# Doubling the recurrence tiles of a hybrid decoder layer, storing branch results in DRAM, and re-tiling its small matrix products

## The chip, the cores and the metric

The kernel runs on one core of a Trainium2 chip. The metric is the device time of one execution in microseconds (us); a time without other words is the median of several executions. A profile is one further execution, recorded instruction by instruction.

## The reference, cut to what matters

One layer on x of 512 tokens by 2048 channels: h = RMSNorm(x), one input projection `h @ w_in` to 57 column tiles of 128, three branches, a SiLU gate on each, one output projection, and the residual.

```python
pa, pb, pc = split(h @ w_in)
# A: RWKV-7, 12 heads of 64; per token t, state S (64 x 64):
#    sa = S @ (-kk_t);  S = S*w_t + outer(sa, kk_t*a_t) + outer(v_t, k_t);  y_t = S @ r_t
#    then group norm of y, plus bonus = sum(r*k*r_k) * v, times silu(ga)
# B: trailing means over 2/4/8/16 tokens minus the token, a 128x128 map per group, a scale, times silu(pg)
# C: stick-breaking attention, 12 heads of 64, QK-norm, strictly causal:
#    z = q @ k.T;  w = exp(log_sigmoid(z) + reversed cumsum of log_sigmoid(-z));  o = w @ v, times silu(g)
out = x + concat(A, B, C) @ w_out
```

## The kernel before

**Layout.** Channels lie on the 128 partitions and the 512 tokens on the free axis. A "pair" is two heads of 64, the lower one (`lo`) on partitions 0 to 63 and the upper one (`hi`) on 64 to 127. There are six pairs for branch A, six for branch C and four groups for branch B.

**Projections.** Each operand of the two big projections is split into a high and a low part of type float32r, and `three` issues three products per block of 128 rows: high-high, high-low and low-high. One column tile of the input projection is thus 16 x 3 = 48 products of 128x128 by 512 columns, into a PSUM bank called `pj`. The first three tiles go into banks called `first` while x arrives; the other 54 tiles follow in a fixed order, eight for a pair (k, r, v, ga, cq, ck, cv, cg), at the end eight for the pooling groups. The output projection is 4 x 4 x 16 x 3 = 768 such products into banks called `oacc`. Weights stream in by half tiles: a 512 KB load (`raw`, two buffers, queue of SyncE, SP), a cast on ScalarE (ACT) that gives `wh`, and a subtraction on VectorE (DVE) that gives `wl`, two buffers each.

**The order on TensorE (PE).** `project` issues the products of one column tile after another, and after each product it calls `pump`. Branches are generators (`rwkv(p)`, `attention(p)`, `pooling(g)`) that stop at `yield need(...)`. A planner (`Pace`) models when each tile will be ready and when a bank of a tag will be free; `pump` resumes a generator once the modelled time has passed that by a margin (MARGIN 1.5 us, TIGHT 0.05 us in the recurrence). Small products of a branch are in this way strewn among the big ones, and all engines work in the order in which they were issued.

**Branch A, pair p.** Decay (`dec`) and rate (`av`) from two products each, the second of which uses 64 rows alone; a sum of squares (`ss`). Chunks of 64 tokens: `bk` holds the keys of the pair and `amr` the decayed keys and receptances. `gm`, four products for each half sequence and head with 64 rows, 128 columns of weights and 128 moving columns, gives the triangles `lt`, `rx` and a part of `amr`. The triangles are inverted: four 32-row pieces go to DRAM, come back so that 128 of them lie on the partitions, a loop of 30 steps on DVE solves them, they go back, and two rounds of 32x32 products (`q`) finish. Then come eight chunks in a row, each with five products per head: `w` (64 output columns of the array), copy to `wsb`, `u` (64x64), copy to `uv`, `s` (64 output columns), the new state into `uv` with the help of `se`, and two products into `y`. A head's product uses its own half of the array. Group norm (`mu`, `var`) and the gate follow. There is one set of `bk`, `amr`, `lt`, `rx`, `ec`, so `rwkv(p)` waits for the end of the recurrence of p-1 before it writes them.

**Branch C, pair p.** QK-norm (`qm`), then per head: scores `z` in three banks, each piece as one product with all 128 rows (high and low part of q stacked) and one with 64 rows (low part of k); an exponential, a scan and POOL's (GpSimd's) masks; ten transposes (`wT`) of the weights into one tile; and four products into `o`, which use 64 output columns.

**Results** of all branches stay in SBUF, one tile each (`yt`), until the output projection, which begins once all tasks but one are done. PSUM banks: two `pj`, three `g` (all phase products), three `c` (recurrence).

Every product is issued by one helper, line 350 (transposes: 354), every DVE, ACT and POOL instruction by line 198, every DMA by line 212 on SP, so rows are told apart by the tiles' names. A float32 product stands as two instructions in the profile, a float32r product and a transpose as one:

```python
pe.matmul(o, lhsT, rhs, start=start, stop=stop)      # line 350, in mm()
pe.transpose(o, src, ident)                          # line 354
call(*args, **kw)                                    # line 198, DVE, ACT and POOL
queue.dma_start(out=out, in_=in_)                    # line 212, SP
```

Of the kernel before, what the change touches and what calls it, by code (L numbers as in the profile page):

```python
# [8 lines left out]
F32 = mybir.dt.float32  # L9
# [4 lines left out]
P = 128  # L14
# [38 lines left out]
BANKS = {"pj": 2, "g": 3, "c": 3}  # L53
MARGIN = 1.5
TIGHT = 0.05
AHEAD = 300
EVACUATE = 25
DL = 4.0


def tile_order():
    tiles = [("wdad", 0)]
    for p in range(NPAIR):
        tiles += [("k", p), ("r", p), ("v", p), ("ga", p)]
        tiles += [("cq", p), ("ck", p), ("cv", p), ("cg", p)]
    for g in range(NPOOL):
        tiles += [("pu", g), ("pg", g)]
    return tiles
# [18 lines left out]
Y_TILE = {("a", i): i for i in range(6)} | {("b", i): 6 + i for i in range(4)} | {("c", i): 10 + i for i in range(6)}  # L87


class Pace:  # L90
# [37 lines left out]
    def cost(self, eng, f, out, ins):  # L128
# [3 lines left out]
        if eng == "pool":  # L132
            if f in ("memset", "affine_select"):
                return 0.05 + n * 0.0011
            return 0.08 + n * (0.0028 if f == "tensor_scalar" else 0.0033)
        if f in ("tensor_scalar", "tensor_copy", "memset") and not any(self.key(a) in self.read_psum for a in ins):
            n *= 0.5
        return 0.065 + n * 0.00104
# [13 lines left out]
    def matmul(self, out, lhsT, rhs):  # L152
        n = self.free(rhs)
        m = self.free(lhsT)
        if rhs.dtype == F32R:
            c = max(n / 2400.0, m * 0.00083)
        else:
            c = max(4 * max(n, 64) / 2400.0, 0.1) * (0.6 if m <= 64 or rhs.shape[0] <= 64 else 1.0)
# [45 lines left out]
def hybrid_trunk_kernel(ctx: ExitStack, tc: tile.TileContext, x, xT, w_in, w_out, vecs, consts, up_w, pool_w, out, tap=None):  # L204
# [15 lines left out]
    tp = ctx.enter_context(tc.tile_pool(name="tp", bufs=14))  # L220
# [57 lines left out]

    hh = [hp.tile([P, T], F32R, tag=f"hh{k}", name=f"hh{k}") for k in range(KT)]
# [14 lines left out]
    for pl, tag, parts in ((ap, "q2", 1), (ap, "k2", 1), (ap, "w3", 1), (rp, "bk", 2), (rp, "bkt", 2), (rp, "rx", 2),  # L294
                           (rp, "uv", 2), (rp, "amr", 3), (ap, "wt", 2)):
        xt = pl.tile([P, parts, T], F32, tag=tag, name=name("x"))
# [15 lines left out]
    def row_sums():  # L312
        for i in range(8):
            xs = yp.tile([P, D // 2], F32, tag="y12" if i % 2 == 0 else "y14", name=name("xs"))
# [43 lines left out]
    def need(*tiles, tag=None, margin=MARGIN):  # L358
        def at():
            t = max([pace.ready.get(Pace.key(a), 0.0) for a in tiles] + [0.0])  # L360
            return margin + (max(t, pace.bank_at(tag, BANKS[tag])) if tag else t)

# [115 lines left out]

    yt = {}
    ypair = {}  # L480

    def ytile(branch, i):
        n = Y_TILE[(branch, i)]
        if n >= 12:
            if n - n % 2 not in ypair:
# [566 lines left out]
```

## Time and profile before

| | |
|---|---|
| median of 3 runs | 1093.07 us (1091.02 to 1093.6) |
| the profiled execution | 1089.68 us, span in the trace 1088.0 us |
| granted TensorE clock, mean | 0.993 |
| busy: PE, DVE, ACT, POOL | 1066.2, 737.6, 427.8, 143.1 us |
| PE instructions | 5552 products, of which 2592 `pj`, 768 `oacc`, 144 `first` |
| DMA | 101.92 MB, mean 94 GB/s |

The span has three stretches: to about 42 us the `first` tiles, to 908 us the input projection with the branches in it, then the output projection. In the middle stretch the work repeats every 130 us, once a pair; 485 to 615 us is one such period. Busy time of PE counts each product until its modelled end, so products overlap in it; what a product costs is read from the starts.

### The profile page before, as it was taken

The numbers are of one execution on the slowest core, as the hardware profiler recorded it, in microseconds if no ns is written. First come the engines' busy times: TensorE is split into PE (matmuls) and PEld (weight loads), VectorE is DVE, ScalarE is ACT, GpSimd is POOL, SyncE is SP. The second block draws the span as 40 slices with busy tenths as digits, with TensorE's granted clock in tenths as the row PEclk, the third lists the DMA queues.
The fourth block names the chain that finished last, engine by engine and source line by source line (L and its number), as shares of the span: only waits on it lengthen the run. The fifth ranks groups of instructions, "written<-read, shape, count | busy, mean of one in ns | idle before, by whom it ended". The sixth has DMA issues, their size and how long they took to land.

```text
span 1088.0 us, 14731 instructions
## 1 busy us (share of the span) xinstructions
PE 1066.2 (98%) x5552; PEld 801.3 (74%) x5552; DVE 737.6 (68%) x1596; ACT 427.8 (39%) x670; POOL 143.1 (13%) x208
## 2 busy tenths in 40 slices
PE   9998999999999999999999999999999999999998
PEld 7877766687666877668766787667776677888887
DVE  6266978759787797778877799777986457223232
ACT  6453525235353354334543345524443235111111
POOL 0031113101132011210211102210021111000000
PEclk9999999999999999899999999999999999999999
DMA  9513231132211321113221132112221125444232
GB/s 329 204 63 105 80 93 40 56 92 84 84 48 51 107 85 66 58 59 97 86 76 39 64 115 77 61 58 84 100 78 55 48 94 163 149 154 137 96 137 75
DMA packets 58185, 101.92 MB, mean 94 GB/s; under 512 B 29312, under 2 KB 30720, under 8 KB 58112
## 3 DMA queue, kind: packets, MB, share of 16 engines
q1 hardware_dynamic: 58112, 100.96, 28.2%
q8 instruction: 44, 0.72, 0.3%
q14 instruction: 29, 0.24, 0.1%
HBM read 95.17 MB, written 5.77 MB: 93 GB/s over the span
## 4 chain that ended last, share of the span: by engine, by line
PE 80%; DVE 10%; issue 4%; ACT 2%; DMA 2%; POOL 2%; SPq 0%; POOLq 0%; DVEq 0%; ACTq 0%
PE pj L350 45%; PE oacc L350 15%; PE first L350 3%; PE o L350 2%; PE z L350 2%; DVE w L198 2%; DVE wl L198 2%; PE gm L350 2%; PE y L350 2%; PE w L350 2%; PE wT L354 1%; DVE xblk L198 1%; PE u L350 1%; POOL e L198 1%; PE s L350 1%
## 5 line engine op out<-in xcount | busy, mean ns | idle before, releaser
L350 PE MATMUL pj<-hl,wh 128*128 128x512 f32 x864 | 349.0, 404 | 0.0
L350 PE MATMUL pj<-hh,wh 128*128 128x512 f32 x864 | 347.9, 403 | 1.0 <-DVE u L198 0.8
L350 PE MATMUL pj<-hh,wl 128*128 128x512 f32 x864 | 347.6, 402 | 0.0
L198 DVE TENSOR_TENSOR wl<-raw,wh 128x1024 fp32r<-128x1024 f32 x140 | 172.1, 1229 | 168.6 <-ACT wh L198 162.8
L198 ACT CAST wh<-raw 128x1024 fp32r<-128x1024 f32 x140 | 147.0, 1050 | 312.7 <-PE pj L350 187.5
L350 PEld LDWEIGHTS pj<-hh,wh 128*128 128x128 f32 x864 | 163.1, 189 | 38.0 <-issue 4.4
L350 PEld LDWEIGHTS pj<-hh,wl 128*128 128x128 f32 x864 | 163.2, 189 | 35.4 <-issue 0.4
L350 PEld LDWEIGHTS pj<-hl,wh 128*128 128x128 f32 x864 | 163.1, 189 | 35.5 <-issue 1.2
L350 PE MATMUL oacc<-wl,yh 128*128 128x512 f32 x256 | 100.1, 391 | 0.8 <-DVE wl L198 0.8
L350 PE MATMUL oacc<-wh,yl 128*128 128x512 f32 x256 | 99.6, 389 | 0.0
L350 PE MATMUL oacc<-wh,yh 128*128 128x512 f32 x256 | 99.6, 389 | 0.0
L198 POOL TENSOR_SCALAR e<-e 128x512 f32<-128x512 f32 x28 | 49.0, 1749 | 327.9 <-ACT e L198 327.6
L198 POOL TENSOR_TENSOR d<-u 128x512 f32<-128x512 f32 x25 | 34.2, 1370 | 230.9 <-DVE u L198 148.6
L350 PEld LDWEIGHTS oacc<-wl,yh 128*128 128x128 f32 x256 | 48.0, 188 | 11.5 <-DVE wl L198 1.3
L350 PEld LDWEIGHTS oacc<-wh,yl 128*128 128x128 f32 x256 | 48.1, 188 | 10.0 <-issue 0.2
L350 PEld LDWEIGHTS oacc<-wh,yh 128*128 128x128 f32 x256 | 48.0, 188 | 10.0
L198 DVE TENSOR_TENSOR xblk<-xblk,pr 128x60 f32<-128x60 f32 (+8 forms) x180 | 44.5, 247 | 4.1
L198 ACT ACTIVATE e<-e 128x512 f32<-128x512 f32 x50 | 31.4, 629 | 39.1 <-POOL e L198 38.8
L198 DVE TENSOR_TENSOR_SCAN w<-kon,n 128x512 f32<-128x512 f32 (+3 forms) x48 | 39.3, 841 | 6.6 <-POOL n L198 6.5
L198 DVE TENSOR_TENSOR pr<-xblk,nblk 128x60 f32<-128x60 f32 (+8 forms) x180 | 38.7, 215 | 4.4
L198 DVE TENSOR_TENSOR u<-pj,rstd 128x512 f32<-128x512 f32 x50 | 34.3, 686 | 8.3 <-PE pj L350 7.9
L198 ACT ACTIVATE n<-n 128x512 f32<-128x512 f32 (+1 forms) x72 | 38.9, 557 | 1.3
(195 smaller groups left out, 1262.7 us busy)
## 6 DMA issues: line engine op xcount, KB each, us to landing
raw<-in_w_in SPq DMA_DIRECT2D x108, 512.0 KB, 3.4
raw<-in_w_out SPq DMA_DIRECT2D x32, 512.0 KB, 3.4
xs<-in_x SPq DMA_DIRECT2D x8, 512.0 KB, 4.7
xr<-in_x SPq DMA_DIRECT2D x16, 256.0 KB, 5.3
out<-xr SPq DMA_DIRECT2D x16, 256.0 KB, 3.2
fr<-in_w_in SPq DMA_DIRECT2D x12, 256.0 KB, 7.4
nblk<-s SPq DMA_DIRECT2D x24, 128.0 KB, 4.9
x<-in_xT SPq DMA_DIRECT2D x5, 512.0 KB, 7.4
```

Source lines behind the costliest of these rows:

```text
L198: return call(*args, **kw)
L350: pe.matmul(o, lhsT, rhs, start=start, stop=stop)
L354: pe.transpose(o, src, ident)
```

## The change

- Two sets of `amr`, `lt`, `bk`, `rx`, `ec` and `bv`, used in turn; `rwkv(p)` waits for the recurrence of p-2 before it writes them, and for that of p-1 only before its own recurrence. `bkt`, `uv`, `yc` stay single.
- `amr` has four 64-column parts a chunk, the third zero on the upper, the fourth zero on the lower partitions; `lt` has a part per head, zero on the other head's partitions. With them `w`, `u`, `s` and both `y` products are one product for both heads with 128 rows and 128 weight columns. `se` moves from DVE to POOL, half of the receptance part too; `wsb` is copied by halves; `y` leaves PSUM once in four chunks.
- `gm`: the products of the two heads alternate, into two banks; `need2` waits for two free `g` banks.
- `dec`, `av`: the second product uses all rows. Its other rows hold the low part of the other operand.
- `z`: the second product uses all 128 rows, with `kl2`, the low part of k on both halves (two POOL copies per head).
- `wT` and `o`: both heads go together, in three groups of columns; the products of the heads alternate.
- `put_away` stores a finished branch result (256 KB, SP queue) in DRAM, except tiles 5 and 15; the output projection loads them back five ahead. The order of its rows is now rwkv 0 to 4, attention 0 to 4, pooling, rwkv 5, attention 5, and it waits for each result by itself, not for all tasks.
- Planner: higher modelled costs for DVE (0.165 us fixed, was 0.065) and POOL, MARGIN 2.5, TIGHT 0.8. Tiles v and ga come after the four attention tiles of the pair. PSUM: two `pj`, three `g`, two `c`, one `y`. 16 work tiles, not 14.

```diff
-BANKS = {"pj": 2, "g": 3, "c": 3}
-MARGIN = 1.5
-TIGHT = 0.05
+BANKS = {"pj": 2, "g": 3, "c": 2, "y": 1}
+MARGIN = 2.5
+TIGHT = 0.8
...
+    def put_away(branch, i):
+        n = Y_TILE[(branch, i)]
+        if n not in Y_ORDER[-2:]:
+            yd[n] = dr.tile([P, T], F32, tag=f"y{n}", bufs=1, name=f"yd{n}")
+            dma(out=yd[n], in_=yt.pop(n))
...
-        mm(dec, upl[lo, 0:P], wd2[lo, :], False, True)
+        mm(dec, upl[:, 0:P], wd2, False, True)
...
-        while p > 0 and not done.get(("rwkv", p - 1)):
+        while p > 1 and not done.get(("rwkv", p - 2)):
...
-        dve.tensor_tensor(amr[:, :, 2, :], r3, e[:, :, 1:], ALU.mult)
+        dve.tensor_tensor(amr[lo, :, 2, :], r3[lo], e[lo, :, 1:], ALU.mult)
+        pool.tensor_tensor(amr[hi, :, 3, :], r3[hi], e[hi, :, 1:], ALU.mult)
...
+            yield need2(*([amr_flat, bk] if half == 0 else []))
+            gs = [gb("gm"), gb("gm")]
+            for j in range(4):
+                cc = 4 * half + j
+                for h, s, other in quad:
+                    mm(gs[h][:, j * P:(j + 1) * P], bk[s, cc, :, :], amr[s, cc, h:4:2, :])
...
-            for h, s, o in quad:
-                mm(wps[s, 0:C], amr[:, cc, h, :], uv[:, cc, h, :])
+            mm(wps, amr[:, cc, 0:2, :], uv[:, cc, :, :])
             wsb = rp.tile([P, C], F32, tag="wsb", bufs=2, name=name("wsb"))
-            dve.tensor_copy(out=wsb, in_=wps[:, 0:C])
+            dve.tensor_copy(out=wsb[lo, :], in_=wps[lo, 0:C])
+            dve.tensor_copy(out=wsb[hi, :], in_=wps[hi, C:P])
...
-                    dve.tensor_scalar(se[s, :], uv[s, cc, h, :], ec[s, cc:cc + 1], None, ALU.mult)
+                    pool.tensor_scalar(se[s, :], uv[s, cc, h, :], ec[s, cc:cc + 1], None, ALU.mult)
...
-            for h, s, o in quad:
-                mm(yps[s, 0:C], uv[s, cc, h, :], amr[s, cc, 2, :], True, False)
-            ups = cb("u")
-            for h, s, o in quad:
-                mm(ups[s, 0:C], lt[s, cc, :], wsb[s, :])
+            mm(ups, lt[:, cc, :, :], wsb)
+            if cc % 4 == 0:
+                ybank = bank("y", "y")
+            yps = ybank[:, (cc % 4) * P:(cc % 4 + 1) * P]
+            mm(yps, uv[:, cc, :, :], amr[:, cc, 2:4, :], True, False)
...
-                for h, s, o in quad:
-                    mm(sps[s, 0:C], bkt[:, cc, h * HD:(h + 1) * HD], uv[:, cc, h, :])
+                mm(sps, bkt[:, cc, :], uv[:, cc, :, :])
...
-            for h, s, o in quad:
-                mm(yps[s, 0:C], uv[:, cc, h, :], rx[:, cc, h, :], False, True)
-            act.copy(out=y[:, cc * C:(cc + 1) * C], in_=yps[:, 0:C])
+            mm(yps, uv[:, cc, :, :], rx[:, cc, :, :], False, True)
...
+            kl2 = ap.tile([P, T], F32R, tag="kl2", name=name("kl2"))
+            pool.tensor_copy(out=kl2[s, :], in_=klo[s, :])
+            pool.tensor_copy(out=kl2[other, :], in_=klo[s, :])
...
-                    mm(z[:, off:off + (i + 1) * P], q2[s, i * P:(i + 1) * P], klo[s, 0:(i + 1) * P], False, True)
+                    mm(z[:, off:off + (i + 1) * P], q2[:, i * P:(i + 1) * P], kl2[:, 0:(i + 1) * P], False, True)
...
-            for j in range(4):
-                mm(o[s, j * P:T], vt[:, j, s], wt[:, pos[j]:pos[j] + T - j * P], j == 0, j == 3)
+            for j in js:
+                for h, s in ((0, lo), (1, hi)):
+                    mm(o[s, j * P:T], vt[:, j, s], parts[h][:, pos[j]], j == 0, j == 2)
...
-    while len(tasks) > 1:
-        pump(True)
...
+    def load_y(i):
+        if i < KT and i not in yin:
+            n = Y_ORDER[i]
+            while not done.get(ready[n]):
+                pump(True)
+            if n in yd:
+                yin[i] = tmp("yin")
+                dma(out=yin[i], in_=yd[n])
+            else:
+                yin[i] = yt[n]
```

## Rows read from the trace of the kernel before

**Rows 1.** Windows: us; PE, PEld, DVE, ACT, POOL busy; clock, DMA share, GB/s

```profile
485.00:615.00 130.00, 128.77 (x722) 93.94 (x720) 104.42 (x240) 55.52 (x93) 20.24 (x30) 1.00 0.24 75
500.00:550.00 50.00, 50.00 (x255) 40.36 (x254) 45.49 (x113) 23.43 (x35) 7.13 (x11) 1.00 0.29 92
```

**Rows 2.** The same view, 485 to 615 us, PE's instructions on `pj` alone

```profile
485.00:615.00 130.00, 100.11 (x386) 1.00 0.24 75
```

**Rows 3.** The chain of waits, its longest piece: start us, length us, what

```profile
920.99 163.28 PE oacc L350 x719
```

**Rows 4.** Timeline of PE (start us, length us): the two products of `dec`

```profile
567.14 0.39 PE L350 MATMUL pj<-hh,wl 128*128 128x512 f32 x1
...
567.71 0.49 PE L350 MATMUL dec<-wd,sl 64*128 64x512 f32 x1
568.13 0.50 PE L350 MATMUL pj<-hh,wh 128*128 128x512 f32 x1
```

**Rows 5.** Timeline of PE: one recurrence step of both heads

```profile
603.13 0.40 PE L350 MATMUL pj<-hh,wh 128*128 128x512 f32 x1
603.46 0.34 PE L350 MATMUL s<-uv,bkt 128*64 128x64 f32 x4
603.62 0.29 PE L350 MATMUL y<-rx,uv 128*64 128x64 f32 x4
603.84 0.50 PE L350 MATMUL pj<-hl,wh 128*128 128x512 f32 x1
604.18 0.40 PE L350 MATMUL pj<-hh,wl 128*128 128x512 f32 x1
```

**Rows 6.** Timeline of PE: four full-size transposes between big products

```profile
579.39 0.39 PE L350 MATMUL pj<-hh,wh 128*128 128x512 f32 x1
579.62 0.60 PE L354 MATMUL wT<-kon,w 128*128 128x128 f32 x4
579.98 0.48 PE L350 MATMUL pj<-hl,wh 128*128 128x512 f32 x1
580.29 0.39 PE L350 MATMUL pj<-hh,wl 128*128 128x512 f32 x1
```

**Rows 7.** Timeline of PE: scores of one head; value products of one head

```profile
526.44 0.40 PE L350 MATMUL pj<-hl,wh 128*128 128x512 f32 x1
527.01 0.49 PE L350 MATMUL z<-klo,q 64*128 64x512 f32 x1
...
529.31 0.50 PE L350 MATMUL pj<-hh,wl 128*128 128x512 f32 x1
...
588.42 2.37 PE L350 MATMUL o<-wt,vt 128*64 128x512 f32 x8
590.72 0.50 PE L350 MATMUL pj<-hh,wh 128*128 128x512 f32 x1
```

**Rows 8.** Timeline of PE: `gm` of one head, and of two heads back to back

```profile
226.01 1.16 PE L350 MATMUL gm<-amr,bk 64*128 64x128 f32 x8
227.10 0.50 PE L350 MATMUL pj<-hl,wh 128*128 128x512 f32 x1
...
485.24 1.71 PE L350 MATMUL gm<-amr,bk 64*128 64x128 f32 x16
486.88 0.50 PE L350 MATMUL pj<-hh,wl 128*128 128x512 f32 x1
```

**Rows 9.** Groups of DVE, 485 to 615 us: count, busy us, mean ns, idle before

```profile
L198 DVE TENSOR_SCALAR se<-uv,ec 64x64 f32<-64x64 f32 x14 | 3.5, 249 | 0.4
L198 DVE COPY uv<-u 64x64 f32<-64x64 f32 x16 | 3.5, 221 | 2.3 <-PE u L350 2.0
```

**Rows 10.** Groups of POOL, 485 to 615 us

```profile
L198 POOL TENSOR_TENSOR y<-u,e 128x512 f32<-128x512 f32 x1 | 1.3, 1287 | 1.3 <-ACT e L198 1.3
L198 POOL COPY ec<-E 128x8 f32<-128x8 f32 x1 | 0.2, 193 | 0.9 <-DVE uv L198 0.9
```

**Rows 11.** Waits of SP's queue (us, times, longest us); landing of weight loads

```profile
SPq L212 <- DVE uv L198: 106.9, 11, 14.2
...
raw<-in_w_in SPq DMA_DIRECT2D x108, 512.0 KB, 3.4
```

More of the change, by code (lines that the diff above doesn't have):

```diff
@@ L58 @@
 DL = 4.0
+TP = 16
 def tile_order():
@@ L361, in at, with need2 @@
             return margin + (max(t, pace.bank_at(tag, BANKS[tag])) if tag else t)
+        return at
+    def need2(*tiles):
+        def at():
+            q = pace.slots.get("g", [])
+            t = max([pace.ready.get(Pace.key(a), 0.0) for a in tiles] + [0.0])
+            free = sorted([pace.read.get(k, 1e9) for k in q] + [0.0] * (BANKS["g"] - len(q)))
+            return MARGIN + max(t, free[1])
         return at
@@ L812, in attention @@
                 act.copy(out=vt, in_=vps.rearrange("p (j c) -> p j c", j=4))
-            wt = ap.tile([P, 1280], F32, tag="wt", name=name("wt"))
-            pos = {}
-            off = 0
-            for js, width in (((0,), 512), ((1, 3), 512), ((2,), 256)):
-                yield need(*blocks.values(), tag="g", margin=MARGIN + 2.0)
+        o = None
+        for js, width in (((0,), 512), ((1, 3), 512), ((2,), 256)):
+            parts = []
+            for h in range(2):
+                yield need(*head[h].values(), tag="g", margin=MARGIN + 2.0)
@@ L818, in attention @@
                 tps = gb("wT")
-                o2 = 0
+                pos = {}
+                off = 0
                 for j in js:
-                    pos[j] = off + o2
+                    pos[j] = slice(off, off + T - j * P)
                     for i in range(j, 4):
-                        transpose(tps[:, o2:o2 + P], blocks[(i, j)])
-                        o2 += P
-                dst = wt[:, off:off + width]
-                (dve.tensor_copy if js[0] != 1 else act.copy)(out=dst, in_=tps[:, 0:width])
@@ L827, in attention @@
-                off += width
-            yield need(wt, vt, tag="g")
-            o = gb("o")
-            for j in range(4):
-                mm(o[s, j * P:T], vt[:, j, s], wt[:, pos[j]:pos[j] + T - j * P], j == 0, j == 3)
-            while ("cg", p) not in got:
-                yield None
-            y = yt[Y_TILE[("c", p)]]
-            dve.tensor_tensor(y[s, :], o[s, :], y[s, :], ALU.mult)
+                        transpose(tps[:, off:off + P], head[h][(i, j)])
+                        off += P
@@ L836, in attention @@
+        while ("cg", p) not in got:
+            yield None
+        y = yt[Y_TILE[("c", p)]]
+        dve.tensor_tensor(y, o, y, ALU.mult)
+        put_away("c", p)
         done[("att", p)] = True
@@ L975, in hybrid_trunk_kernel @@
             dma(out=out[tb * P:(tb + 1) * P, nb * 512:(nb + 1) * 512], in_=xr)
-    if tap is not None:
-        for i in range(KT):
-            dma(out=tap[i], in_=yt[i])
 def _pack(inputs):
```

234 lines of the change are left out of this document (130 added, 104 removed).

## The prediction

> **What bounds the kernel now.** I read the windows first. In one pair's period PE is busy for 128.77 of 130.00 us, DVE for 104.42, POOL for 20.24 [rows 1]. PE leaves 1.2 us idle, DVE 25.6, so what PE issues sets the end. A busy PE tells nothing of what a product costs, so I go by starts. In the chain's longest piece 719 big products take 163.28 us, 0.227 us each [rows 3]. The period holds 386 products of `pj` [rows 2], 386 x 0.227 = 87.6 us. So 130.0 - 1.2 - 87.6 = 41.2 us of PE's time per pair go to small products, and these the change rewrites.
>
> The timeline tells what a small product costs, as the extra distance between big ones. One step of `s` and `y`, eight instructions, stretches two intervals to 604.18 - 603.13 = 1.05 us [rows 5]; less 2 x 0.227 it costs 0.60. Only 603.84 - 603.46 = 0.38 of that lies between its first start and the next big product; about 0.10 is lost going in (0.33 from the big product to `s` where 0.227 is usual) and 0.11 after (0.34 to the second big product). Each change of the array's shape thus waits for the work inside. Four full-size transposes between big products stretch two intervals to 0.90 [rows 6] and cost 0.90 - 0.45 = 0.45, or 0.11 each, with no loss going in (0.23). Where a stretch is known only to the first big product after it, I add the 0.11.
>
> **The change, part by part**, per pair, on PE.
>
> *Recurrence.* What it costs now is a remainder. Out of the 41.2 go: scores 2 x 2.75 (529.31 - 526.44 - 0.227 + 0.11 [rows 7]) = 5.5; value products 2 x 2.5 (2.30 to the next big product [rows 7], 0.10 before, 0.11 after) = 5.0; `gm` 4.45 (below); `dec` and `av` 2 x 0.87 (568.13 - 567.14 - 0.227 + 0.11 [rows 4]) = 1.75; unchanged 36 transposes x 0.11 = 4.0 and 12 wide float32r products x 0.23 = 2.8; and two blocks of 32x32 products, an estimate of 2.0 from two shape changes of 0.42 (0.60 less eight instructions, [rows 5]) and 64 narrow instructions. That leaves 15.7 us, 1.96 per chunk. After the change a chunk has five full-size float32 products, ten instructions (eight in the last chunk), of 128 weight columns; nothing in the trace has just this form, and I take the 0.11 of a full-size transpose, as it moves the same number of columns: 78 x 0.11 = 8.6. `u` streams 64 columns and could cost half of this; that bounds it from below at 7.7. Two passes a column instead of one would bound it above at 17. I stay at 0.11, as the 64-row `gm`, a true float32 product with 128 columns, also advances by 0.11: 1.09 us from its first start to the next big product [rows 8], less 0.2 for the way out, over eight instructions. Saving 7.1.
>
> *Scores.* Eight products with all rows cost their columns, 2 x (512 + 384 + 128 + 256) / 512 x 0.227 = 1.14, or 1.3 as the narrow ones hardly fall below 0.11. With 2.75 now, 2 x 1.45 = 2.9 saved. Above, half the shape losses could stay: 2.0.
>
> *Values.* Column halves of the two heads run side by side: `s` and `y` of both heads, eight instructions, took 0.38 us with their start-up [rows 5]. One pair's 1280 columns then cost what one head's cost, 2.1, and three groups pay three shape changes of 0.40: 3.3, against 5.0. If the heads did not overlap it would be 2 x 2.1 + 1.2 = 5.4. I take 3.3, saving 1.7.
>
> *`gm`.* One head's eight instructions take 1.09 us to the next big product, sixteen of two heads back to back 1.64 [rows 8]: the second eight add 0.55 where eight at 0.11 would be 0.9, so row halves do overlap where they meet. Now one stretch of sixteen and two of eight: 1.85 + 2 x 1.30 = 4.45. Alternating, sixteen cost what eight do: 2 x 1.30 = 2.6. Saving 1.85 (nothing if they went one by one).
>
> *`dec`, `av`.* 2 x (0.87 - 0.45) = 0.84.
>
> Sum 7.1 + 2.9 + 1.7 + 1.85 + 0.84 = 14.4 us per pair, 86.4 for six pairs; a pair then takes 115.6.
>
> *Other engines.* DVE loses `se`, 3.5 us, and gains eight copies of 0.22 as `wsb` is halved [rows 9], 1.8; fewer gate products and copies take about 1 us more off. So 101.7 in 115.6 us, 88%. In the first part of the period it was at 45.49 of 50 us, 91%, while PE was busy throughout [rows 1]; so this can be borne, but results come later in busy stretches. I add half of today's 1.2 us of PE idle per pair: +4 in all (between -7, all waits gone, and what the first rival costs). POOL gets 14 x `se` (between 0.19 [rows 10] and DVE's 0.25 [rows 9]), four copies of `kl2` and half the receptances at some 1.29 each [rows 10]: 10 us on 20, covered by its idle time; if it is late, `se` holds the next state back, and DVE's `uv` behind it. ACT gets a copy of `bn` and one of `wT` more a pair, and half the evictions of `y`: nothing, hidden in 74 us idle.
>
> *Waits and queues.* TIGHT and MARGIN add 0.75 to 1 us to each of three stops in a chunk, some 20 us per recurrence; big products fill it, and pair p+1 may prepare meanwhile. If that cover were gone, it would cost up to 20 us, once, at the end, where now the eight pooling tiles stand, 8 x 48 x 0.227 = 87 us. One recurrence bank fewer costs nothing, as a chunk's `w`, `u`, `s` share one. `gm` wants two of the three `g` banks at once, and `o` keeps one through three groups: the planner lets big products pass meanwhile, and a bank that comes free late is in the +4. Eight POOL clears at the start lie before the first `gm`: nothing, or some 8 x 1.29 [rows 10] = 10 us of POOL alone. SP issues 14 stores and 14 loads of 256 KB more: 7.3 MB on 102, and DMA is at a quarter of its time [rows 1]. A store waits on SP for the gate product on DVE with weight loads queued behind it; second rival. The reload begins five tiles ahead, 2.5 x 24 x 0.227 = 14 us, against a landing of 3.4 us for twice the size [rows 11]: nothing. The new order of the output rows and dropping the final drain of tasks: nothing; if the last results came late, PE would wait between `pj` and `oacc`.
>
> The profiled execution took 1089.68 us, 3.4 less than the median of 1093.07. By it: 1089.7 - 86.4 + 4 = 1007.3; as a median 1010.7, so 1011 us.
>
> **Rivals.**
>
> *DVE becomes the bound.* It works in order, and in the period it idles 130.0 - 104.4 = 25.6 us [rows 1], in which it may stand behind an instruction that waits. If all that stayed, a pair took 101.7 + 25.6 = 127.3 us, and the gain would be 2.7 x 6 = 16: 1077 us; with half of it PE stays the bound. For it: 88% is high for an engine in order. Against: the stretch at 91%. Chance 0.10. POOL's added 10 us could also block DVE in full, 111.7 of 115.6. The Trainium skill, SBUF — State Buffer, section "SBUF: two separate sides", says that GpSimd and a DVE instruction with two SBUF inputs hold a shared port pair in turn, never both; by that, moving `se` to POOL frees DVE of less than its 3.5 us.
>
> *Weight loads come late behind stores.* Slower than before. SP once stood 14.2 us behind a DVE result [rows 11]. The second `raw` buffer covers a half tile, 24 x 0.227 = 5.4 us. If each of the 14 stores stood so long, 14 x 8.8 = 123 us: 1134. The gain is eaten from 82 / 14 + 5.4 = 11.3 us a store on. Against: such waits exist now, yet PE idles 1.2 us in 130. Chance 0.05.
>
> *Half-array products are the cheaper form.* The two heads run side by side today; full-size products stream twice the columns for zeros. If shape changes were not what costs, the 20 instructions of a chunk would stand for about 0.5 us of stream and ten full-size ones for 1.1: +0.6 x 48 = 29; scores and `dec` would gain nothing, values and `gm` 21: 1093 + 29 - 21 = 1101. Rows 5 speak against it: 0.21 us of 0.60 lie in the changes of shape. The Trainium skill, TensorEngine Tiling (Array Packing), section "Theoretical Speedup", promises up to twofold for dimensions of at most 64, which is this rival's side; its section on properties adds that a change of tiling mode drains the engine. The trace sides with the latter. Chance 0.02.
>
> *The heads don't overlap* in `o` and `gm`: +2.1 x 6 + 1.85 x 6 = 24: 1035. Chance 0.03.
>
> **How the numbers follow.** The forecast has 0.80. Its own bounds: 16 half-price instructions of `u` (5 us) and no PE wait at all (11) give 995; a few us of less broken stretches in the first pairs, where no period is regular, 990. Above, scores with half their losses (12) and the start of DVE's rival give 1050. So 990 to 1050 leaves out most of the first rival and the two slow cases. A measurement tells 0.3%, 3 us, from no change. Faster: 0.80 + 0.10 + 0.03 and a little of the rest, 0.94; same 0.02; slower 0.04.
>
> **What would show it.** Right: the pair's period at 115 to 117 us with PE still over 97% busy; `w`, `u`, `s`, `y` as 128*128 with starts 0.11 apart and no loss going in; scores of a head within 1.4 us; `gm` and `o` starting in twos. Wrong: PE waits on DVE `uv` or `wl` of more than 2 us a pair (first rival); SP waits on the gate and PE waits on `wl` in the same place (second); full-size products 0.2 apart (upper bound of the recurrence).

## The result, and the profile after

The changed kernel takes **1124.43 us** (median of 4 runs, 1120.82 to 1124.78), the kernel before beside it 1092.05 us: ratio 1.0291, 95% interval 1.0261 to 1.032. It is slower by 32 us; 1011 us, faster, had been forecast. The profiled execution has a span of 1123.1 us, its mean granted clock is 0.941 (0.993 before). Ratios compare undisturbed executions; one of the four of run a1 below ran throughout at a granted clock of 0.56, took 1629.75 us and is left out.

The page of the changed kernel: PE's busy time, PE and its granted clock in 40 slices of 28 us, and the chain that ended last, by engine.

```profile
PE 1023.5 (91%) x5084; PEld 818.0 (73%) x5084; DVE 733.7 (65%) x1554; ACT 427.2 (38%) x658; POOL 228.0 (20%) x330
...
PE   8989999899989999999999989999986067999998
PEclk9999999999999999998999999999995555999999
...
PE 54%; DVE 21%; issue 9%; ACT 6%; POOL 5%; DMA 4%; SPq 0%; DVEq 0%; POOLq 0%; ACTq 0%
```

PE's busy time fell from 1066.2 to 1023.5 us, yet the span grew by 35: its idle time rose from 21.8 (1088.0 - 1066.2) to 99.6 us. The reader sees a hole near the end of PE's line, with the clock at half beneath it. PE holds 54% of the chain, DVE 21%.

The windows of the changed kernel, one period of a pair and then the end (columns as in [rows 1], which they answer), and behind them the first of these stretches for the products of `pj` alone, which answers [rows 2].

```profile
519.90:670.70 150.80, 144.67 (x764) 115.75 (x763) 116.39 (x251) 65.88 (x104) 34.02 (x49) 0.98 0.25 83
...
824.00:949.00 125.00, 66.00 (x284) 46.97 (x284) 56.50 (x192) 16.11 (x30) 16.64 (x31) 0.56 0.10 28
```

```profile
519.90:670.70 150.80, 124.50 (x484) 0.98 0.25 83
```

From the `gm` of one pair to that of the next it is now 150.8 us where it was 130, and in this time 484 products of `pj` pass, not 386: ten column tiles, where a pair owns eight. The pairs of the branches fall behind the input projection. When that has run out, pair 4's recurrence but for its first chunk and the rest of pair 5's chain are still to come, with little beside them: 125 us in which PE is busy for 66.0, at a clock of 0.56.

The timeline of PE where the input projection ends, and the piece of the chain with which the output projection begins in earnest (start us, length us, what; it answers [rows 3]).

```profile
823.83 0.39 PE L367 MATMUL pj<-hh,wl 128*128 128x512 f32 x1
824.05 0.33 PE L367 MATMUL wus<-wsb,lt 128*128 128x64 f32 x2
```

```profile
949.12 170.24 PE oacc L367 x744
```

So the account closes. The input projection ends at 824.05 us instead of 908.0: 84.0 earlier. Then come 125.1 us until 949.12, in which only 768 - 744 = 24 of the output products find a place. The rest takes 174.0 us (1123.1 - 949.1) where the whole took 180.0 (1088.0 - 908.0). -84.0 + 125.1 - 6.0 = +35.1, the difference of the spans. The 84.0 looks like the forecast's 82.4 but isn't a saving of that size, since most of pair 4's recurrence and pair 5's chain from `gm` on were not done by then, only put off.

**The products that were read became as cheap as forecast.** The timeline of PE in the changed kernel: scores of one head, a recurrence step, `gm` of two heads, the first group of value products.

```profile
567.27 0.39 PE L367 MATMUL pj<-hl,wh 128*128 128x512 f32 x1
567.49 0.39 PE L367 MATMUL z<-k,q 128*128 128x512 f32 x1
...
568.77 0.39 PE L367 MATMUL pj<-hh,wl 128*128 128x512 f32 x1
...
386.41 0.39 PE L367 MATMUL var<-sl,bmean_r 128*128 128x512 f32 x1
386.63 0.38 PE L367 MATMUL wus<-uv,bkt 128*128 128x128 f32 x2
386.85 0.39 PE L367 MATMUL y<-rx,uv 128*128 128x128 f32 x2
...
387.31 0.40 PE L367 MATMUL pj<-hh,wh 128*128 128x512 f32 x1
...
817.05 0.39 PE L367 MATMUL pj<-hl,wh 128*128 128x512 f32 x1
817.36 1.16 PE L367 MATMUL gm<-amr,bk 64*128 64x128 f32 x16
...
818.79 0.39 PE L367 MATMUL pj<-hh,wh 128*128 128x512 f32 x1
...
741.55 0.40 PE L367 MATMUL pj<-hh,wh 128*128 128x512 f32 x1
741.88 1.08 PE L367 MATMUL o<-wt,vt 128*64 128x512 f32 x4
...
743.23 0.39 PE L367 MATMUL pj<-hh,wl 128*128 128x512 f32 x1
```

Scores: 568.77 - 567.27 - 0.227 = 1.27 us (forecast 1.3; they answer [rows 7]). The step, four instructions: 387.31 - 386.41 - 0.45 = 0.45, 0.11 each (forecast 0.11; [rows 5]), and 0.22 from the `var` before to the first of them, so no loss going in. `gm` of sixteen: 818.79 - 817.05 - 0.45 = 1.29 (forecast 1.3; [rows 8]). First group of `o`: 743.23 - 741.55 - 0.45 = 1.23, where 3.3 was forecast for all three; the other two, and `dec`, were not read. The Trainium skill, TensorEngine Tiling (Array Packing), section "Key Properties", says that a change of tiling mode drains the array; the trace agrees, as the scores, now without one, lose nothing going in (567.49 - 567.27 = 0.22).

**What is late is the recurrence.** From the start of its first product to the end of its last it took 54 to 65 us per pair before, and in the changed kernel 121 to 161 us in pairs 0 to 3, which run beside the input projection. The first and the last product in pair 2, after and then before (timeline of PE):

```profile
513.70 0.38 PE L367 MATMUL wus<-uv,amr 128*128 128x128 f32 x2
...
645.87 0.38 PE L367 MATMUL y<-rx,uv 128*128 128x128 f32 x2
```

```profile
419.06 0.34 PE L350 MATMUL w<-uv,amr 128*64 128x64 f32 x4
...
477.70 0.34 PE L350 MATMUL y<-rx,uv 128*64 128x64 f32 x4
```

A hand-over has two parts, which can be summed over a recurrence from the starts and ends in the traces (pairs 0 to 3). From PE's product to DVE's result it was 26 to 28 us before and is 56 to 86 us now: DVE has other work ahead in its queue. From DVE's result to PE's next product of the chain it was 18 to 22 us and is 53 to 66 us: this is what the planner lets pass on PE first. The timeline of DVE inside one chunk of pair 2; `pr` and `xblk` are the solver of pair 3.

```profile
566.30 0.21 DVE L205 COPY uv<-wus 64x64 f32<-64x64 f32 x1
566.43 1.23 DVE L205 TENSOR_TENSOR pr<-xblk,nblk 128x48 f32<-128x48 f32 x1
567.69 0.23 DVE L205 COPY uv<-wus 64x64 f32<-64x64 f32 x1
...
575.90 1.22 DVE L205 TENSOR_TENSOR_SCAN w<-kon,n 128x512 f32<-128x512 f32 x1
...
583.33 0.30 DVE L205 TENSOR_TENSOR xblk<-xblk,pr 128x70 f32<-128x70 f32 x1
583.56 0.78 DVE L205 SCALAR_TENSOR_TENSOR d<-d,vec,u 128x512 f32<-128x512 f32 x1
584.27 1.21 DVE L205 TENSOR_TENSOR wl<-raw,wh 128x1024 fp32r<-128x1024 f32 x1
585.54 0.27 DVE L205 SCALAR_TENSOR_TENSOR uv<-wus,ec,se 64x64 f32<-64x64 f32 x1
585.97 0.29 DVE L205 SCALAR_TENSOR_TENSOR uv<-wus,ec,se 64x64 f32<-64x64 f32 x1
```

The values are in `uv` at 567.92; PE issues `s` at 572.20, and DVE forms the next state from it at 585.54. Between them DVE is not idle: it works through the other pair's solver (6.4 us), scans and scores (6.1), weight parts (3.4) and smaller things, in the order of its queue. One of the three hand-overs of this chunk takes 18 us in this way, 4.3 of them before PE issues `s`. Over a whole recurrence of pairs 0 to 3 the next pair's solver takes 12 to 15 us of DVE, of the 93 to 128 us that DVE works in it.

The waits of PE in the changed kernel (us in total, times, longest us):

```profile
PE q L367 <- DVE xt L205: 33.3, 2, 32.7
PE wus L367 <- DVE uv L205: 15.1, 25, 2.0
```

The 32.7 us are pair 5's solver at the end, with its ways to DRAM and back; PE has nothing else to do beside it.

### The profile page after: what moved, and what is told of

Read it like the earlier page. It is cut to its first block, busy times and chain, and to the rows that moved or that the text cites. A ratio compares the mean times of both kernels' runs of the same rounds, so it can differ in the third digit from the quotient of the medians.

```text
span 1123.1 us, 13956 instructions
## 1 busy us (share of the span) xinstructions
PE 1023.5 (91%) x5084; PEld 818.0 (73%) x5084; DVE 733.7 (65%) x1554; ACT 427.2 (38%) x658; POOL 228.0 (20%) x330
## 4 chain that ended last, share of the span: by engine, by line
PE 54%; DVE 21%; issue 9%; ACT 6%; POOL 5%; DMA 4%; SPq 0%; DVEq 0%; POOLq 0%; ACTq 0%
PE pj L367 26%; PE oacc L367 16%; DVE wl L205 4%; PE wus L367 4%; POOL e L205 3%; DVE w L205 3%; DVE xblk L205 2%; ACT e L205 2%; DVE pr L205 2%; DVE uv L205 2%; PE first L367 1%; ACT wh L205 1%; PE y L367 1%; DVE u L205 1%; PE o L367 1%
## 5 line engine op out<-in xcount | busy, mean ns | idle before, releaser
L205 DVE TENSOR_TENSOR wl<-raw,wh 128x1024 fp32r<-128x1024 f32 x140 | 175.8, 1256 | 137.6 <-ACT wh L205 137.1
L367 PEld LDWEIGHTS pj<-hh,wl 128*128 128x128 f32 x864 | 164.2, 190 | 44.1 <-DVE wl L205 11.5
L205 POOL TENSOR_SCALAR se<-uv,ec 64x64 f32<-64x64 f32 x84 | 45.4, 541 | 220.8 <-DVE uv L205 202.8
L205 POOL TENSOR_SCALAR e<-e 128x512 f32<-128x512 f32 x28 | 45.4, 1622 | 123.5 <-ACT e L205 101.9
L205 POOL TENSOR_TENSOR d<-u 128x512 f32<-128x512 f32 x25 | 36.5, 1461 | 79.0 <-DVE u L205 52.3
L205 DVE TENSOR_TENSOR xblk<-xblk,pr 128x60 f32<-128x60 f32 (+8 forms) x180 | 41.4, 230 | 5.3
```

The lines of the kernel that those rows point to most:

```text
L205: return call(*args, **kw)
```

## The experiments

Ratios are to the kernel before on the same chip, with 95% intervals; where there is none (a2, a3, a4), the kernel ran once.

**Which part of the change makes the end run alone?**

*a1.* The planner's fixed DVE cost as before; all else changed.

```diff
-        return 0.165 + n * 0.00104
+        return 0.065 + n * 0.00104
```

> One number of the changed kernel goes back: the planner's fixed cost of a DVE instruction, 0.065 us and not 0.165; no instruction is added or removed, only their order may move. Theory P (the planner counts DVE as nearly full, so it spreads a recurrence over some ten column tiles, longer than the eight that a pair brings, and the last pair and a half run after the last big product): the recurrences end before the input projection does, the gap of some 110 us before the output projection goes, and the time is 1000 to 1030 us. Theory Q (DVE itself, in order, holds the recurrence up behind the next pair's solver): the recurrence steps still wait on DVE, PE stalls at them instead, and the time stays above 1080 us.

Measured 1104.6 us, 1.0102 (1.0062 to 1.0142). The hole is gone (`oacc` starts at 920.7 us), as theory P said, but the time stays where theory Q had it: the recurrences of pairs 0 to 4 take 113 to 119 us, and PE now waits throughout: in a period of 127.5 us it is busy for 117.5. What the end gave back was largely lost in the middle.

*a2.* MARGIN and TIGHT as before, the rest changed.

```diff
-MARGIN = 2.5
-TIGHT = 0.8
+MARGIN = 1.5
+TIGHT = 0.05
```

> Of the changed kernel MARGIN and TIGHT alone go back to 1.5 and 0.05. Theory P: the margins add 0.75 us to each of 24 stops of a recurrence, some 18 us of 130, and the gap shrinks by one or two tenths: 1090 to 1115 us. Rival M (the margins are what makes the recurrence long): the gap goes, 1000 to 1040 us.

Measured 1101.08 us, within theory P's range; a hole stays (from 845 to 925 us PE is busy for 49.7 us). The margins are worth about 23 us of the time, yet they are not what makes the recurrence long: it still takes 122 to 150 us in pairs 0 to 3, and from DVE's results to PE's next products there still pass 59 to 69 us.

*a3.* The late results last among the output rows.

```diff
-Y_ORDER = [0, 1, 2, 3, 4, 10, 11, 12, 13, 14, 6, 7, 8, 9, 5, 15]
+Y_ORDER = [0, 1, 2, 3, 10, 11, 12, 13, 14, 15, 6, 7, 8, 9, 4, 5]
```

> Of the changed kernel the order of the output projection's rows alone is changed: rwkv 4 and 5 come last, so that the output products may start while their recurrences are open. Theory P: the work in the gap is the same, but up to 7/8 of the first output quarter, 38 us, can run beside it: 1080 to 1095 us. Rival O (the gap is made by the forced drain ahead of the output alone): the gap goes, about 1020 us.

Measured 1123.27 us, nothing gained, against both expectations: `oacc` starts at 826 us and 204 output products, not 24, are done before the late chain ends, but pair 5's recurrence then ends at 977 us rather than 941. The length of the chain decides, not the order of the rows.

*a4.* The solver stops for the planner after each of its 30 steps, not each sixth.

```diff
-            if j % 6 == 0:
-                yield soon(xblk)
+            yield soon(xblk)
```

> Of the changed kernel the solver of the next pair stops after each of its 30 steps, not after each sixth, so that DVE has two of its instructions, not twelve, ahead of a recurrence step. Theory Q: a recurrence in the middle shortens from 130 to below 100 us and the time falls below 1080 us. Theory P: the planner spreads the steps as before, the recurrence stays above 115 us and the time within 1105 to 1130 us.

Measured 1134.69 us, recurrences of 121 to 132 us in pairs 0 to 3: finer pieces of the solver don't help. This speaks against theory Q, and the time lies a little above what theory P allowed.

**Does the overlap of pairs do it, or the planner?**

*b1.* No overlap: `rwkv(p)` waits for p-1 as before, the old tile order, planner costs and margins; the new products, stores and row order stay.

```diff
-        while p > 1 and not done.get(("rwkv", p - 2)):
+        while p > 0 and not done.get(("rwkv", p - 1)):
...
-        tiles += [("k", p), ("r", p)]
-        tiles += [("cq", p), ("ck", p), ("cv", p), ("cg", p)]
-        tiles += [("v", p), ("ga", p)]
+        tiles += [("k", p), ("r", p), ("v", p), ("ga", p)]
+        tiles += [("cq", p), ("ck", p), ("cv", p), ("cg", p)]
...
-MARGIN = 2.5
-TIGHT = 0.8
+MARGIN = 1.5
+TIGHT = 0.05
...
-        return 0.165 + n * 0.00104
+        return 0.065 + n * 0.00104
...
```

> The changed kernel with all that sets its order put back: pair p waits for the recurrence of p-1, the tiles v and ga come before attention, the planner has its old costs and margins. The new products, the DRAM results and the new row order stay. Theory D (the saving on PE is real, 14 us a pair, but the pairs' overlap and the planner's new numbers give it back as waits for DVE): a pair takes 115 to 122 us and the time is 1000 to 1045 us. Rival N (DVE's handing over in order bounds the pair at some 127 us whatever the order): 1065 us or more, with PE waits on DVE of 10 us a pair.

Measured 1094.56 us, 1.0018 (1.0002 to 1.0033). These are the prediction's cheaper products in the old order, without the overlap, and they bring nothing: PE's idle time is 71.8 us, and the recurrences take 35 to 51 us, less than before.

*b2.* The overlap and the new tile order kept; all planner costs (DVE, POOL and PE) and margins as before, as in b1; the cut shows DVE's.

```diff
-MARGIN = 2.5
-TIGHT = 0.8
+MARGIN = 1.5
+TIGHT = 0.05
...
-        return 0.165 + n * 0.00104
+        return 0.065 + n * 0.00104
...
```

> Of the changed kernel the planner's costs and margins go back, the overlap of two pairs stays. Theory D with the planner as the main part: 1000 to 1050 us. Theory D with the overlap as the main part: recurrences are issued densely but wait on DVE behind the next pair's solver, 1070 to 1110 us.

Measured 1094.99 us, 1.0012 (0.9988 to 1.0035): the same. So the new planner numbers, together, are what makes the changed kernel slower than before. They are also what makes the recurrences long: here these take 56 to 77 us in pairs 0 to 3, with the overlap in place, and from pair 1 on none of the next pair's solver falls into them. But something else keeps the 82 us away. PE's line of the page, in a span of 1093.2 us:

```profile
PE 1022.7 (94%) x5084; PEld 805.8 (74%) x5084; DVE 740.1 (68%) x1554; ACT 429.4 (39%) x658; POOL 232.4 (21%) x330
```

PE's idle time is 70.5 us where it was 21.8. The mean granted clock is 0.978 where it was 0.993, which as an estimate is another 16 us of full-speed time (0.022 x 1093.2 less 0.007 x 1088.0).

*b3.* b2, and the solver of pair p waits until the recurrence of p-1 is over.

```diff
+        while p > 0 and not done.get(("rwkv", p - 1)):
+            yield None
         nblk = rp.tile([P, B, B], F32, tag="bk", bufs=2, name=name("nblk"))
```

> As the run with the old planner, and the solver of pair p waits for the recurrence of p-1, so that of the overlap only the steps up to the triangles stay. If the solver's instructions on DVE are what holds the recurrence up: 30 us or more below the run with the old planner alone, near 1010 to 1040 us. If not: within 15 us of it.

Measured 1083.48 us, 0.9902 (0.9866 to 0.9939), 11.5 us below b2. By its own expectation this is the case in which the solver on DVE does not hold the recurrence up: the recurrences of pairs 0 to 4 take 65 to 68 us, against 49 to 77 in b2, where only pair 0's had any of the solver in it (10 us). The next three runs build on it.

*c1.* b3 with the changed kernel's MARGIN.

```diff
-MARGIN = 1.5
+MARGIN = 2.5
```

> The run that put the solver after the recurrence, with MARGIN at 2.5 for the stops outside the recurrence (TIGHT stays 0.05, old costs). Theory D: what is left of PE's waits there (on xt, wt, masks, sums: the planner resumes too early as it counts DVE too cheaply) goes, the granted clock stays up, the recurrences still end before the last big product: 1045 to 1070 us. Rival N (the chain of one pair sets the period): the waits move or the chain lengthens, 1078 us or more.

Measured **1074.11 us, 0.9841 (0.9813 to 0.9869)**, the best of the versions that compute everything, and faster than both kernels. It lies between the two ranges expected. Windows of one period in b3 and in c1, and the longest of c1's waits of PE:

```profile
437.40:563.70 126.30, 119.12 (x643) 92.51 (x643) 101.24 (x233) 55.40 (x90) 37.34 (x49) 1.00 0.27 81
```

```profile
465.10:592.60 127.50, 119.65 (x644) 93.56 (x643) 101.04 (x231) 56.39 (x91) 36.02 (x49) 0.99 0.26 80
```

```profile
PE wus L365 <- DVE wsb L203: 16.9, 13, 1.9
PE wus L365 <- DVE uv L203: 14.0, 19, 1.8
```

The period is near 127 us in both, 7 to 8 us of it without PE; in the kernel before PE idled 1.2 of 130 [rows 1].

*c2.* b3 with `se` back on DVE.

```diff
-                    pool.tensor_scalar(se[s, :], uv[s, cc, h, :], ec[s, cc:cc + 1], None, ALU.mult)
+                    dve.tensor_scalar(se[s, :], uv[s, cc, h, :], ec[s, cc:cc + 1], None, ALU.mult)
```

> The run that put the solver after the recurrence, with se on DVE as before. If POOL's 0.54 to 0.6 us a piece and its queue hold the next state up: 5 to 20 us less than the same run with POOL, 1063 to 1078 us. If DVE's load counts for more: 3.5 us a pair more of DVE, up to 20 us more.

Measured 1097.16 us, 1.0038 (1.0019 to 1.0056), 14 us above b3. DVE's busy time rises from 732.1 to 755.9 us. The move of `se` to GpSimd, which the prediction booked as 3.5 us of DVE per pair beside other work, is worth 14 us on the end, the planner's order having moved with it.

*c3.* c1 with the planner's new costs for PE's products.

```diff
-            c = max(n / 2400.0, m * 0.00083)
+            c = max(n / 2400.0 + 0.010, 0.19 * m / 128)
...
-            c = max(4 * max(n, 64) / 2400.0, 0.1) * (0.6 if m <= 64 or rhs.shape[0] <= 64 else 1.0)
+            c = max(4 * max(n, 64) / 2400.0, 0.214 if m > 64 else 0.1) * (0.6 if m <= 64 or rhs.shape[0] <= 64 else 1.0)
```

> As the run with MARGIN 2.5, with the planner's new, longer costs of PE's products. It then thinks PE later than with the old ones, so stops are resumed after fewer big products. Theory D: steps come earlier against DVE and PE waits more: 5 to 20 us above the run with the old product costs. If waits do not depend on that: within 4 us.

Measured 1098.15 us, 1.0058 (1.0035 to 1.0081), 24 us above c1, from three numbers in the planner, with the same instructions in another order.

**Is a cheaper product worth anything in the kernel before?**

*b4.* The kernel before with full rows for `dec`, `av` and the scores alone (with the two copies into `kl2`).

```diff
-        mm(dec, upl[lo, 0:P], wd2[lo, :], False, True)
+        mm(dec, upl[:, 0:P], wd2, False, True)
...
-                    mm(z[:, off:off + (i + 1) * P], q2[s, i * P:(i + 1) * P], klo[s, 0:(i + 1) * P], False, True)
+                    mm(z[:, off:off + (i + 1) * P], q2[:, i * P:(i + 1) * P], kl2[:, 0:(i + 1) * P], False, True)
```

> The kernel before with two parts of the change alone: the second products of dec, av and of the scores use all 128 rows (with kl2 by POOL). By the prediction's terms PE is spared 0.84 + 2.9 = 3.7 us a pair: if PE sets the end, 22 us less, 1068 to 1074 us. If DVE takes it back: 1080 to 1092 us.

Measured 1126.64 us, 1.0298 (1.0266 to 1.033): 33 us slower, where its own terms in the sum, 2.9 + 0.84 us a pair, make 22 us faster. The timeline of PE shows how (the bracket is idle time and what ended it), and the window behind the wait:

```profile
289.70 1.07 PE L350 MATMUL q<-xt,lt 32*32 32x32 f32 x32 [3.88 <-DVE xt L198]
...
300.08 0.63 PE L350 MATMUL pj<-hl,wh 128*128 128x512 f32 x1
300.51 0.63 PE L350 MATMUL pj<-hh,wl 128*128 128x512 f32 x1
```

```profile
289.70:308.30 18.60, 18.60 (x117) 12.27 (x118) 8.28 (x18) 4.02 (x8) 1.04 (x1) 0.50 0.20 64
```

PE arrives early at a product that waits 3.88 us for DVE, and the big products after it start 0.43 us apart where 0.227 is usual: the window says half the clock until 308 us, 18.6 us in which PE is busy throughout. The wait is thus paid again in the clock. Over the kernel PE's idle time rises by 28 us (50.1 against 21.8), and the mean clock of 0.961 costs some 36 us more than the 0.993 of the kernel before, as an estimate; with the 22 us spared this makes +42, and the spans differ by 39.5.

*c4.* b4 with MARGIN 2.5.

```diff
-MARGIN = 1.5
+MARGIN = 2.5
```

> The kernel before with the full rows of dec, av and scores, which alone came out 3% slower, now with MARGIN 2.5. Theory D (resuming too early costs PE waits, after which the granted clock is at its lower level for microseconds): waits and low clock shrink and the spared 3.7 us a pair begin to show, 1065 to 1090 us. Rival: the extra POOL copies or DVE itself hold it, 1105 us or more.

Measured 1102.85 us, 1.011 (1.0076 to 1.0144): 24 us better than b4, though less than expected and still above the kernel before. PE's idle time hardly changes (47.7 us); the mean clock does, to 0.984. Here and in c1 a wider MARGIN pays; in the changed kernel MARGIN and TIGHT cost 23 us together (a2), and no run moved TIGHT alone.

**Is it DVE's load, or what stands in its queue?** Three runs leave the solver's loop out:

```diff
-        for j in range(1, B - 1):
+        for j in range(1, 2):
```

*d1*, from c1:

> This is c1_wider_stops with the loop of the triangular solver cut from 30 steps to one, so the solution of the 32 by 32 blocks is left out (some 58 VectorE instructions of 0.23 us per pair, 14 us of VectorE per pair, 85 us in all). Theory H (the pair is set by hand-overs through a VectorE that runs in order and is 80% busy, so that TensorE waits for it): VectorE falls from 100 to 86 us per pair, the pair of 126.5 us comes down by 5 to 12 us, and the time lands at 1000 to 1045 us. Rival R (the pair is set by TensorE's own 118 us and the granted clock; VectorE's load beside it is hidden): 1064 to 1076 us.

*d2*, from the kernel before:

> The kernel before with the same loop cut to one step (same part left out). In the kernel before TensorE holds 80% of the chain of waits and VectorE 10%. Theory H: the gain is smaller than in d1, 1065 to 1088 us, since TensorE's work per pair (some 120 us of 130) leaves less to win; if the gain is as large as in d1 or larger, the kernel before was as much bound by VectorE as the changed one, and the prediction's reading of the old chain was the mistake. Rival R: 1085 to 1092 us.

*d3*, from the changed kernel:

> The changed kernel itself with the same loop cut to one step (same part left out); its order of work still puts the last pair's recurrence behind the last input projection. Theory H: the solver of the next pair no longer stands in VectorE's queue between the steps of a recurrence, so each recurrence shortens from some 130 us by 14 us or more and the idle stretch of TensorE at the end shrinks: 1050 to 1100 us. Rival R (the order alone, not VectorE's queue, leaves the last pairs to the end): 1110 to 1124 us.

Measured: d1 1066.77 us, 0.9755 (0.9729 to 0.978); d2 1110.91 us, 1.0168 (1.013 to 1.0207); d3 **1042.38 us, 0.9532 (0.9514 to 0.9549)**. The windows, of d2 (one period) and d3 (four periods, then the products of `pj` in them):

```profile
477.40:609.40 132.00, 130.63 (x721) 94.39 (x720) 91.02 (x182) 55.66 (x92) 24.01 (x30) 1.00 0.24 73
```

```profile
195.30:674.80 479.50, 455.21 (x2507) 367.22 (x2506) 356.51 (x676) 216.90 (x349) 138.96 (x192) 0.99 0.27 82
```

```profile
195.30:674.80 479.50, 386.61 (x1497) 0.99 0.27 82
```

In d2 DVE has 13 us less to do in a period than in [rows 1], and the period does not shrink, so DVE's load does not bound the kernel before. But the kernel became 17 us slower, which no expectation allowed: with 58 instructions a pair gone the planner orders the rest otherwise, and the mean clock is 0.981. In d1 7 us go from c1, within rival R's range: DVE's load alone is not the bound there, and theory H fails.

In d3 82 us go from the changed kernel, more than any expectation allowed. Its four periods take 119.9 us each with 374 products of `pj`; the forecast was 115.6 with the 386 of [rows 2], and 12 products more at 0.227 would make it 122.6, as an estimate. The input projection ends at 853.1 us with no long hole behind it; the recurrences of pairs 0 to 4 still take 104 to 124 us. So a long recurrence can be borne while enough big products stand beside it, and even without the solver's work the 1011 us forecast for all of the work is not reached. What d3 can't separate: it takes 68 us off DVE, and the planner's order changes when 58 instructions a pair are gone. That the solver's place in DVE's queue makes the difference is thus not shown.

**The solver on another engine.** *d4*, all of the work kept:

```diff
-            dve.tensor_tensor(prv, xblk[:, 0:ni, j:j + 1].to_broadcast([P, ni, m]),
+            pool.tensor_tensor(prv, xblk[:, 0:ni, j:j + 1].to_broadcast([P, ni, m]),
...
-            dve.tensor_tensor(xblk[:, 0:ni, j + 1:B], xblk[:, 0:ni, j + 1:B], prv, ALU.add)
+            pool.tensor_tensor(xblk[:, 0:ni, j + 1:B], xblk[:, 0:ni, j + 1:B], prv, ALU.add)
```

> The changed kernel with the solver's two instructions per step (product and sum, 360 in all) on GpSimd instead of VectorE; all of the computation stays. Theory H (the solver in VectorE's queue between the steps of the other pair's recurrence is what makes the recurrences long): VectorE loses 14 us per pair as in d3, but the order still ends with the last recurrence behind the last input projection, and GpSimd is slower per instruction: 1060 to 1110 us. If the solver only moves the wait to the scaled copy se, which runs on GpSimd behind it, the time stays at 1110 to 1150 us. Rival R (the order alone): 1115 to 1130 us.

*d5*, d4 with the old planner costs (DVE's among them):

```diff
-        return 0.165 + n * 0.00104
+        return 0.065 + n * 0.00104
...
```

> d4 with the planner's costs of the kernel before, so that the last recurrence starts before the last three input projections. Theory H: as d3, 1040 to 1080 us. If se waits behind the solver on GpSimd: 1085 to 1110 us. Rival R: about the 1095 us of b2_old_planner.

*d6*, d5 with `se` on DVE, the edit of c2:

> d5 with the scaled copy se on VectorE, so that nothing of the recurrence stands behind the solver on GpSimd. VectorE wins 14 us per pair from the solver and takes back 14 small instructions of some 0.2 us, 3 us. If the hand-over through GpSimd behind the solver costs, this is the faster of the two, by 10 us or more, 1035 to 1070 us; if not, it is 0 to 14 us slower than d5.

Measured 1131.98, 1141.59 and 1146.35 us (1.038, 1.0465, 1.0509; each within 0.004). Theory H's times are all missed; d4 lies where waiting behind the solver on GpSimd was expected, d6 within the 14 us above d5 that were expected if `se` does not matter. What the traces do show is how a queue in order loses time. Waits of DVE and PE in d4, and the timeline of DVE at one of them:

```profile
DVE xblk L205 <- POOL pr L205: 86.5, 11, 18.9
...
PE wus L367 <- DVE wsb L205: 46.7, 7, 15.8
```

```profile
412.14 0.60 DVE L205 SCALAR_TENSOR_TENSOR uv<-wus,ec,se 64x64 f32<-64x64 f32 x2 [0.28 <-PE wus L367]
427.36 0.07 DVE L205 MEMSET xblk<- 32x8 f32 x1 [14.63 <-POOL pr L205]
...
431.82 0.45 DVE L205 COPY wsb<-wus 64x64 f32<-64x64 f32 x2
```

The solver's arithmetic has left DVE, whose busy time falls to 662.9 us; but four small clears of `xblk` stayed in its queue, and at the first DVE stands for 14.63 us with the recurrence's copies behind it. DVE is idle there, and the recurrences of pairs 0 to 4 take 119 to 133 us. In such a wait it isn't DVE's load that costs; it is what stands ahead in its queue. That `se` waits behind the solver on GpSimd is not what costs: d6 is no faster than d5. Moving the clears too wasn't tried, and how much of the changed kernel's loss is of this kind no run shows.

## Why the prediction was wrong

**Right:** the price of each product that could be read off, within 0.1 us for the scores, the step, `gm` and the first group of `o`. PE's busy time fell accordingly. What the cheaper products saved in all can be estimated from the spans less the added idle time and the lower clock: some 86 us in d3, some 60 in b2, against a forecast of 86.4. The second rival did not occur: PE waits for `wl` 6.8 us in all and 1.9 at most. The third and fourth fall with the rows shown above. That PE's work bounds the kernel before is half confirmed: DVE's load doesn't (d2), but taking work off PE alone did not help either (b1, b4, c4).

**The step that failed** is the one on waits: "TIGHT and MARGIN add 0.75 to 1 us to each of three stops in a chunk, some 20 us per recurrence; big products fill it", with a cost of "up to 20 us, once, at the end", and the "+4 in all" for waits. In place of the +4, PE's idle time rises by 49 us in b2, where the planner is that of before, and the lower clock takes some 16 us more: this eats the saving. In the changed kernel it rises by 78 us. Four things were wrong in it.

- *The size.* The recurrence grew by 61 to 96 us, not by 20, and not by the margins: with both back (a2) it is still 122 to 150 us long, with all of the planner's numbers back (b2) 56 to 77. A margin is only the earliest time at which a step may be issued; it then joins DVE's queue behind all that was issued before it. The prediction counted the overlap as a benefit ("pair p+1 may prepare meanwhile") and never asked what stands ahead in DVE's order; the next pair's solver is 12 to 15 us of it.
- *The cover.* Big products do fill the waits, but they are a stock: eight tiles a pair, 87 us of PE. A chain of 121 to 161 us per pair eats ten tiles, and the stock is gone before the chains are. The prediction had the place right, the end, and priced it at one recurrence's extra 20 us; there were 125 us, at a clock of 0.56.
- *The planner.* Its costs were listed as part of the change and then given no term. All of its numbers together make 29 us (b2 against the changed kernel); c3 shows 24 us from three of them, a1 20 us from one.
- *The output.* The new order of its rows was put at nothing. From the last product of `pj` to the end it took 180.2 us before and 187 to 188 us in b1, b2, c1 and d3; `oacc` begins some 6 us after `pj`, 4.8 of them a wait for `yh` of ACT.

**The first rival** was nearer than the forecast, at its chance of 0.10. With the hole mended (b3, c1) the period is near 127 us, its formula's 127.3; c1's 1074 us is near its 1077. But that is luck, as c1 is another kernel than the one forecast, and its reason, DVE's load plus a fixed idle time, does not hold: d1 takes 10 us of DVE's time from the period and the time falls by 7 us in all. The prediction also leaned on DVE's 91% in 500 to 550 us as a proof that such a load can be borne. PE had work throughout that stretch; it says nothing of one in which PE has to wait for DVE.

The Trainium skill, SBUF — State Buffer, section "SBUF: two separate sides", was cited for a shared port by which moving `se` would free DVE of less than its time. c2 does not show that: DVE's busy time differs by 23.8 us for 84 instructions, 0.28 us each, where one took 0.25 us [rows 9]. It is no test of the rule either, as b2 and b3, with the same instructions, differ by 8.0 us.

**Open:** what makes DVE hand over late. The solver in its queue is one candidate, for which d3 speaks; against it speak a4, b2 and b3, and no run moved the solver and kept the order of all else. Open too is why c1 and d1 stay near 128 us a pair where d3 runs at 120. The recurrences are dense in the first two, 42 to 80 us against 104 to 124 in pairs 0 to 4; no run varied that alone.

## What to carry to other kernels

When one engine is full and the others nearly so, a sum of the full engine's savings holds only while every chain that runs beside it is shorter than its share of cover: compare the chain's length per period with the cover's, before and after. For each step of such a chain, list what stands ahead of it in every in-order queue that it passes, work of other tasks and mere waits alike; an overlap that helps one task can lengthen that list for the other. And read a planner's constants as part of the program: here they moved 20 to 29 us without adding or removing an instruction.

## What was unexpected of the hardware

A few microseconds of waiting on TensorE cost a multiple here. In b4 a wait of 3.88 us was followed by products 0.43 us apart until about 308 us, the level of 1.2 GHz, where 0.227 is usual. In the changed kernel's hole at the end, in pair 4's recurrence (the timeline of PE)

```profile
851.89 0.80 PE L367 MATMUL wus<-uv,bkt 128*128 128x128 f32 x2 [0.64 <-DVE uv L205]
852.48 0.64 PE L367 MATMUL y<-rx,uv 128*128 128x128 f32 x2
853.46 0.77 PE L367 MATMUL wus<-uv,amr 128*128 128x128 f32 x2 [0.34 <-DVE uv L205]
```

the clock is at 0.50 while PE waits only 0.3 to 0.6 us at a time between small products, so that a chain with no cover pays for each product more than twice: two instructions stand 0.59 us before the next where 0.22 is usual. The kernel before shows the same once in its middle, after a wait of 1.2 us for DVE `uv` (window of all engines):

```profile
443.00:449.00 6.00, 6.00 (x24) 3.79 (x23) 4.15 (x13) 3.92 (x7) 2.08 (x3) 0.50 0.01 3
```
